# Which buffer a result may take, and the order of the last row tiles, in a one-core hybrid attention trunk

## The chip, the core and the metric

The kernel runs on one core of a Trainium2 chip. A core has five engines with a queue each: TensorE (PE; weight loads are shown apart as PEld), VectorE (DVE), ScalarE (ACT), GpSimd (POOL) and SyncE (SP). Here SP issues all loads and the stores of the output, and POOL issues the stores of intermediate results to DRAM. Each queue works in the order that the program gives it. Data lie in SBUF (128 partitions) and, for matmul results, in PSUM banks. The metric is the device time of one execution in microseconds (us); less is better. "Before" was timed in three runs, and one more execution was profiled.

## What is computed

One layer of a decoder trunk on 1024 tokens of 1024 channels, float32. A normalised input h goes through one wide projection, and its parts feed two recurrent branches, which are gated, merged and projected back:

```
h = rms_norm(x, norm_w) * (1 + scale) + shift          # scale, shift, gate from c
hq, hf, hi, hz, gq, gk, gv, gz, ga, mg = split(h @ w_in)
y_h = hgrn2_branch(hq, hf, hi, hz, ...)                # 8 heads of 128
y_g = gla_branch(gq, gk, gv, gz, ga, ...)              # 4 heads, keys 128, values 256
u_h, u_g = y_h @ w_branch[0], y_g @ w_branch[1]
merged = sigmoid(mg[0]) * u_h + sigmoid(mg[1]) * u_g
x = x + gate * (merged @ w_out)
out = rms_norm(x, final_norm_w)
```

Both branches are gated linear attentions, `S_t = diag(a_t) S_{t-1} + k_t v_t^T`, `o_t = S_t^T q_t`, computed in chunks.

## The kernel before

**Precision and slots.** Large matmuls run on pairs: each operand is split into a rounded high part (ACT, `copy` to fp32r) and the rest as low part (DVE, `tensor_sub`), and three products are summed (`split`, L195 to 202). Nearly everything large lives in 46 equal buffers of SBUF, 4 KB a partition each, which the class `Slots` hands out: loads, split parts, features, states. `get` takes the first slot of a heap; `free` puts a slot back with the running number of the takings as its key, so that the slot returned longest ago is taken first. A slot is returned when the program text is done with it, not when the hardware is: the framework then makes the next writer of that slot wait for whatever still reads or writes it. Some slots are returned right after the issue of a store that reads them; they are returned with `sent=True`, and in the last stages only (`S.behind = 8`, L1694) their key is put eight takings back. `Halves` (`Q`) hands out half slots.

**Order.** In the opening (up to `order.close()`, L450) TensorE, ACT and DVE work in the order of the text. Behind it the framework plans the order: it goes through the instructions by an estimate of its own and issues on each engine what is ready, the earlier in the text first. `tc.keep_in_program_order` ties an instruction behind the one that stands before it in the text on the same engine.

**Stages.**

- The opening: the norm of x, the modulation vector, and the first projections of GLA's queries and keys.
- The stream (`Stream`, L861; `stream.go()`, L1692): some 40 jobs, each a block of the input projection (`Feat`, L551; `Vblk`, L570; `Vblk2`, L614), in order. A job's weights are loaded two jobs ahead and split one ahead (`ahead`). Its result leaves PSUM through `silu_done` (L953, with L956 on ACT and L957 on DVE), `hf_done` (L1081) or copies of values (L609, L652). Between the matmuls of the jobs, `weave` places pieces of two side tracks: the attention of each head (`attention`, L661; keys turned into `kT`, L805 to 812; states, L833 to 840; outputs, L852 to 854; the square of the output, L985, and for GLA a row sum by matmul with ones, L961 to 972, L968 and L969), and preparation for the last stages: differences of the activations (`factors`, L1162) and sums of weight blocks (`weight_sums`, L1190: two loads x1 and x2 at L1196, two result slots s1 and s2 at L1199, four additions at L1202 to L1206, four stores on POOL at L1208). Finished GLA heads are scaled (L998) and stored by `put_act` (L918, L920).
- The last stages (`last_stages`, L1397, matmuls at L1351): gates and branch outputs by Strassen-like products of blocks (seven products per 2 x 2 block).
- The output stage (`out_stage`, L1585, matmuls at L1528): the output projection, again by seven products (1, 5, 3, 6, 7, 2, 4), each over four row tiles i. Row tiles 4 to 7 are closed behind product 7, row tiles 0 to 3 behind products 2 (first 512 columns) and 4 (last 512 columns).

**The end of a row tile.** `first_columns` sums the squares of the first half (ACT, accumulator into `sso[:, t, 0]`) and multiplies with the norm weight. `last_columns` (L1542) adds the product to the row (DVE, L1544), sums the squares of the second half (L1536), adds both sums (DVE, L1547), takes the root on ACT (L1548) and the reciprocal on DVE (L1549), then scales the first half on ACT (L1550) and the second on DVE (L1552), and stores both halves from SP (L1551, L1553). All of it for one tile stands in the text ahead of the next tile.

Of the kernel before, what the change touches and what calls it, by code (L numbers as in the profile page):

```python
# [10 lines left out]
F32 = mybir.dt.float32  # L11
# [24 lines left out]
class Slots:  # L36


    def __init__(self, pool, n):
        self.pool = pool  # L40
        self.free_list = [(-1, i - n, i) for i in range(n)]
        self.freed = self.behind = 0
        self.owner = {}
        self.serial = 0

    def get(self, shape, dtype=F32):
        i = heapq.heappop(self.free_list)[-1]
        self.serial += 1
        t = self.pool.tile([P] + list(shape), dtype, tag=f"s{i}", name=f"b{self.serial}")
        self.owner[id(t)] = (i, t)  # L50
        return t

    def free(self, *tiles, sent=False):
        for t in tiles:
            self.freed += 1
            heapq.heappush(self.free_list, (self.serial + (self.behind if sent else 0), self.freed, self.owner.pop(id(t))[0]))


# [29 lines left out]
def hybrid_trunk_kernel(  # L88
# [106 lines left out]
    def split(src, hi=None, lo=None):  # L195

        if hi is None:
            hi = S.get(list(src.shape[1:]), F32R)
            lo = S.get(list(src.shape[1:]), F32R)
        nc.scalar.copy(hi, src)  # L200
        nc.vector.tensor_sub(lo, src, hi.bitcast(F32))  # L201
        return hi, lo
# [326 lines left out]

    def split_feat(lw):  # L530
        raw, w = lw
        hi = S.get([KT, P], F32R)
        lo = S.get([KT, P], F32R)
        split(raw[:, :, 0:w], hi[:, :, 0:w], lo[:, :, 0:w])
        S.free(raw)
        return hi, lo
# [33 lines left out]
    class Vblk:  # L570
# [14 lines left out]
        def prep(self):  # L585
            self.wt = []
            for b in self.raw:
                hi = S.get([4, 256], F32R)
                lo = S.get([4, 256], F32R)
                split(b, hi, lo)  # L590
                self.wt.append((hi, lo))
                S.free(b)

        def run(self):
            v = [S.get([4, 256]) for _ in range(2)]
            for g in range(2):
                ps = dtile()
                for i in range(4):
                    t = g * 4 + i
                    for k in range(KT):  # L600
                        hi, lo = self.wt[k // 4]
                        lh, ll = h_hi[k][:, t * P:(t + 1) * P], h_lo[k][:, t * P:(t + 1) * P]
                        o = ps[:, i * 256:(i + 1) * 256]
                        nc.tensor.matmul(o, lh, hi[:, k % 4, :], start=(k == 0), stop=False)  # L604
                        nc.tensor.matmul(o, lh, lo[:, k % 4, :], start=False, stop=False)  # L605
                        nc.tensor.matmul(o, ll, hi[:, k % 4, :], start=False, stop=(k == KT - 1))  # L606
                        if k % 4 == 3:
                            yield
                nc.scalar.copy(v[g].rearrange("p a b -> p (a b)"), ps)  # L609
            for hi, lo in self.wt:  # L610
                S.free(hi, lo)
            self.done(v)

    class Vblk2:  # L614
# [18 lines left out]
                S.free(b)  # L633

        def run(self):
            v = [S.get([2, 512]) for _ in range(4)]
            for g in range(4):
                if g == 2:
                    self.middle()
                ps = dtile()  # L640
                for i in range(2):
                    t = 2 * g + i
                    o = ps[:, i * 512:(i + 1) * 512]
                    for k in range(KT):
                        hi, lo = self.wt[k // 2]
                        lh, ll = h_hi[k][:, t * P:(t + 1) * P], h_lo[k][:, t * P:(t + 1) * P]
                        nc.tensor.matmul(o, lh, hi[:, k % 2, :], start=(k == 0), stop=False)  # L647
                        nc.tensor.matmul(o, lh, lo[:, k % 2, :], start=False, stop=False)  # L648
                        nc.tensor.matmul(o, ll, hi[:, k % 2, :], start=False, stop=(k == KT - 1))
                        if k % 2:  # L650
                            yield
                nc.scalar.copy(v[g].rearrange("p a b -> p (a b)"), ps)  # L652
            for hi, lo in self.wt:
                S.free(hi, lo)
            self.done(v)
# [5 lines left out]
    def attention(q, k, f, v, vo, V, post, lead=3):  # L661
# [140 lines left out]
        yield 3.5  # L802


        kT = S.get([NCH, P])  # L805
        for g in range(2):
            nt = 4 if g == 0 else 3
            pt = mtile()
# [114 lines left out]
    def alpha_side():  # L923
        lower_bound()
        for h0 in (0, 2):
            zs = {}
            for h in (h0, h0 + 1):
                zb, m = S.get([T]), S.get([T])
                for th in range(2):
                    pz = mtile()  # L930
                    nc.tensor.matmul(pz, aw4[:, h * P:(h + 1) * P], ga4[:, th * 512:(th + 1) * 512],
                                     start=True, stop=True)
                    nc.scalar.activation(zb[:, th * 512:(th + 1) * 512], pz, AF.Identity,
                                         bias=vec[:, R_AB + h:R_AB + h + 1])
                tc.keep_in_program_order(nc.vector.tensor_scalar_min(m, zb, 0.0))
                nc.vector.scalar_tensor_tensor(zb, m, 2.0, zb, ALU.mult, ALU.subtract)
                zs[h] = zb
                alphas[h] = m
                yield 9 if h == 0 else 2
            for zb in zs.values():  # L940
                nc.scalar.activation(zb, zb, AF.Exp)
            yield 4
            for h, zb in zs.items():
                nc.scalar.activation(zb, zb, AF.Ln, bias=one_t)
                nc.vector.tensor_sub(alphas[h], alphas[h], zb)
            yield 4
            for h, zb in zs.items():
                nc.scalar.activation(alphas[h], alphas[h], AF.Exp, scale=1.0 / TAU)
                S.free(zb)
            yield 4  # L950
        S.free(ga4, aw4)

    def silu_done(store, key):  # L953
        def f(ps):
            s = S.get([T])
            nc.scalar.activation(s, ps, AF.Sigmoid)  # L956
            nc.vector.tensor_mul(s, s, ps)  # L957
            store[key] = s
        return f
# [14 lines left out]
    def gla_attention(h):  # L974
        qk = g_state
        v = qk.pop(("v", h))
        g = {}
        sq = {}

        def post(vh, half, po):  # L980
            if half == 0:
                g[vh] = qk.pop(("z", h, vh))
                sq[vh] = S.get([T])
            sl = slice(half * 512, half * 512 + 512)
            nc.scalar.activation(sq[vh][:, sl], po, AF.Square)  # L985
            nc.vector.scalar_tensor_tensor(g[vh][:, sl], po, vec[:, R_GN + vh:R_GN + vh + 1],
                                           g[vh][:, sl], ALU.mult, ALU.mult)

        yield from attention(qk.pop(("q", h)), qk.pop(("k", h)), alphas[h], lambda: v, 0, 256, post)
        S.free(*v)  # L990
        nc.vector.tensor_add(sq[0], sq[0], sq[1])
        yield 1.5
        rst = sq[1]
        yield from inverse_root(rst, sq[0], 256)
        for half in range(4):
            sl = slice(half * 256, half * 256 + 256)
            for vh in range(2):
                nc.vector.tensor_mul(g[vh][:, sl], g[vh][:, sl], rst[:, sl])  # L998
            yield 1.5
        for vh in range(2):  # L1000
            put_act(yg_d, 2 * h + vh, g[vh])
        S.free(*sq.values())

    def gla_k_done(h):
        def f(ps):
            t = S.get([T])
            nc.vector.tensor_copy(t, ps)
            g_state[("k", h)] = t
        return f
# [70 lines left out]

    def hf_done(h):  # L1081
        def fn(ps):
            f, k = S.get([T]), S.get([T])
            nc.scalar.activation(f, ps, AF.Sigmoid)
            nc.scalar.activation(k, ps, AF.Sigmoid, scale=-1.0)
            nc.vector.tensor_scalar(f, f, oml[:, h:h + 1], lb[:, h:h + 1], ALU.mult, ALU.add)
# [6 lines left out]
    def hgrn_attention(h):  # L1093
# [21 lines left out]
            S.free(sq[0])  # L1115
        if h == 7:
            yield 2
            rst = S.get([T])
            yield from inverse_root(rst, ssq[0], D)
            S.free(ssq[0])  # L1120
            rst_h[0] = rst
# [40 lines left out]
    def factors(acts, f):  # L1162
        sub = nc.vector.tensor_sub
        for kk in range(2):
# [1 line left out]
                yield 1  # L1166
            y = {}
            for b in ("12", "11", "22", "21"):
                y[b] = S.get([T])
                nc.sync.dma_start(y[b], part_of(acts, int(b[0]) - 1, int(b[1]) - 1, kk))  # L1170
            yield 6
            for p, dst, a, b in ((5, "11", "12", "11"), (7, "12", "12", "22"), (6, "22", "22", "11"), (4, "21", "21", "22")):
# [17 lines left out]
    def weight_sums(b, i):  # L1190
# [5 lines left out]
            nc.sync.dma_start(x.rearrange("p k a f -> p k (a f)"),  # L1196
                              src[kh * 512:(kh + 1) * 512, :].rearrange("(k p) f -> p k f", p=P))
        yield 6
        s1, s2 = S.get([2, 4, P]), S.get([2, 4, P])  # L1199
        parts = {5: s1[:, 0], 6: s1[:, 1], 3: s2[:, 0], 7: s2[:, 1]}  # L1200
        add = nc.vector.tensor_add
        add(parts[7], x1[:, :, 0], x1[:, :, 1])  # L1202
# [327 lines left out]

    nj = [0]

    def squares(t, f, src):
        nj[0] += 1
        junk = xb_f[:, nj[0] % 4 * 512:nj[0] % 4 * 512 + 512]
# [19 lines left out]
    def out_after(p, i):  # L1555
# [22 lines left out]
            Q.free(snap4.pop(i))  # L1578
        elif p == 2:
            first_columns(i, bank4["c", i])  # L1580
            R.free(bank4.pop(("c", i)))
        elif p == 4:
            last_columns(i, bank4["b", i])

    def out_stage():  # L1585
        for p in OUT_PRODUCTS:
# [141 lines left out]
```

## Time and profile before

| what | value |
|---|---|
| median of 3 runs | 1210.58 us (1209.76 to 1211.31) |
| the profiled execution's own time | 1208.55 us |
| its span, first to last instruction | 1206.8 us |
| granted TensorE clock, mean | 0.999 |
| DMA, mean over the span | 152 GB/s, 183.51 MB |
| SP's waits for a slot still in use, longest in total | 57.8 us (L1282, matmuls of L1351), 13 times |

All stretches named below are in us from the start of the span. A wait "A <- B" means that A's engine stood idle until B was done. In operand names the buffer numbers are left out: every slot is `b`, PSUM tiles are `pd`, `pm` and `sc_ps`; `yg`, `ws` and `fx` are DRAM copies of activations, weight sums and differences. The ends of matmuls are modelled, and idle time of an engine that isn't the bottleneck costs nothing by itself.

### The profile page before, as it was taken

To read this page: it belongs to the slowest core of one execution; us is meant where nothing else is said; L and a number is where in the kernel's file an instruction comes from. 1 tells how busy PE (TensorE), PEld (TensorE's weight loads), DVE (VectorE), ACT (ScalarE), POOL (GpSimd) and SP (SyncE) were. 2 spreads that over 40 slices of the span, in tenths; PEclk is the share of its full clock that TensorE was granted. 3 is DMA by queue.
4 is the path that set the end of the run, shared out by engine and by line. 5 is a ranking of instruction groups with operands and counts; after the bars stand their busy time and mean duration, and the time that the engine had idled before them with its cause. 6 is when DMAs were issued, how large, how long until landed. Compare 5 with 4: busy or idle time off the path is not lost.

```text
span 1206.8 us, 20832 instructions
## 1 busy us (share of the span) xinstructions
PE 1179.6 (98%) x8575; PEld 982.2 (81%) x8575; DVE 793.2 (66%) x1258; ACT 548.4 (45%) x798; POOL 95.2 (8%) x204
## 2 busy tenths in 40 slices
PE   5999999999999999999999999999999999999997
PEld 3777889889898888888888888877888888878886
DVE  5637444774947556877975365795653866988994
ACT  5646732434434244334333324464743644444554
POOL 4100000101101021011100000001120000000000
PEclk9999999999999999999999999999999999999999
DMA  9814000844444267255342212155797846435523
GB/s 323 278 70 140 18 19 19 292 146 159 158 152 153 59 206 255 93 175 170 121 175 54 70 36 71 36 175 168 248 349 248 279 155 209 125 107 172 177 101 124
DMA packets 130960, 183.51 MB, mean 152 GB/s; under 512 B 7467, under 2 KB 97633, under 8 KB 130866
## 3 DMA queue, kind: packets, MB, share of 16 engines
q1 hardware_dynamic: 117250, 136.87, 36.2%
q0 software_dynamic: 13568, 45.31, 9.7%
q8 instruction: 67, 1.10, 0.4%
q14 instruction: 27, 0.22, 0.1%
q10 hardware_dynamic: 48, 0.01, 0.0%
HBM read 132.87 MB, written 49.28 MB: 151 GB/s over the span
## 4 chain that ended last, share of the span: by engine, by line
PE 47%; issue 39%; POOL 3%; DMA 2%; DVE 2%; ACT 2%; SPq 0%; POOLq 0%; ACTq 0%; DVEq 0%
PE pd L1351 9%; PE pd L545 9%; PE sc_ps L1351 5%; PE pm L1351 5%; PE pd L1528 3%; PE pd L606 2%; PE pd L605 2%; PE pd L604 2%; POOL ws L1208 2%; PE sc_ps L1528 2%; DMA b<-in_w_in_dram 2%; PE pd L356 1%; PE pm L1528 1%; PE pm L852 1%; PE pm L854 1%
## 5 line engine op out<-in xcount | busy, mean ns | idle before, releaser
L545 PE MATMUL pd<-b,b 128*128 128x512 f32 x1632 | 387.4, 394 | 0.0
L545 PEld LDWEIGHTS pd<-b,b 128*128 128x128 f32 x1632 | 302.4, 188 | 64.8 <-issue 1.4
L1351 PE MATMUL pd<-b,b 128*128 128x512 f32 x720 | 173.6, 392 | 2.4 <-DVE b L957 1.0
L1351 PEld LDWEIGHTS pd<-b,b 128*128 128x128 f32 x720 | 133.9, 188 | 33.4 <-ACT b L1422 1.9
L201 DVE TENSOR_TENSOR b<-b,b 128x1024 fp32r<-128x1024 f32 (+2 forms) x90 | 97.9, 1097 | 71.1 <-ACT b L200 57.5
L200 ACT CAST b<-b 128x1024 fp32r<-128x1024 f32 (+2 forms) x90 | 84.2, 949 | 92.6 <-PE pd L545 13.7
L1294 DVE TENSOR_TENSOR b<-b,b 128x1024 fp32r<-128x1024 f32 x56 | 68.3, 1221 | 56.2 <-ACT b L1293 35.3
L1293 ACT CAST b<-b 128x1024 fp32r<-128x1024 f32 x56 | 58.7, 1051 | 64.6 <-PE pm L1351 20.0
L1351 PE MATMUL sc_ps<-b,b 128*128 128x512 f32 x324 | 79.3, 391 | 1.5 <-ACT scT L797 1.5
L604 PE MATMUL pd<-b,b 128*128 128x256 f32 x256 | 74.2, 290 | 0.0
L1351 PEld LDWEIGHTS sc_ps<-b,b 128*128 128x128 f32 x324 | 60.3, 188 | 15.1 <-ACT scT L797 1.9
L1272 DVE TENSOR_TENSOR b<-b,b 128x1024 fp32r<-128x1024 f32 x48 | 57.7, 1219 | 22.5 <-ACT b L1271 14.0
L606 PE MATMUL pd<-b,b 128*128 128x256 f32 x256 | 72.5, 283 | 0.0
L605 PE MATMUL pd<-b,b 128*128 128x256 f32 x256 | 72.4, 283 | 0.0
L1351 PE MATMUL pm<-b,b 128*128 128x512 f32 x300 | 72.1, 389 | 0.0
L1271 ACT CAST b<-b 128x1024 fp32r<-128x1024 f32 x48 | 49.9, 1051 | 36.6 <-PE pd L1351 16.0
L1351 PEld LDWEIGHTS pm<-b,b 128*128 128x128 f32 x300 | 56.3, 188 | 11.7
L356 PE MATMUL pd<-b,b 128*128 128x512 f32 x192 | 53.1, 409 | 1.8 <-ACT b L200 0.9
L1208 POOL DMA_DIRECT2D ws<-b x64 | 34.6, 540 | 224.8 <-DVE b L1202 121.7
L739 ACT COPY xb<-b 128x512 f32<-128x512 f32 x48 | 29.4, 620 | 48.9 <-PE sc_ps L719 26.8
L647 PE MATMUL pd<-b,b 128*128 128x512 f32 x128 | 51.2, 400 | 0.0
L648 PE MATMUL pd<-b,b 128*128 128x512 f32 x128 | 50.0, 390 | 0.0
(286 smaller groups left out, 1935.9 us busy)
## 6 DMA issues: line engine op xcount, KB each, us to landing
b<-in_w_in_dram SPq DMA_DIRECT2D x66, 512.0 KB, 4.3
ws<-b POOLq DMA_DIRECT2D x64, 256.0 KB, 3.4
b<-ws SPq DMA_DIRECT2D x32, 512.0 KB, 3.8
b<-in_x_dram SPq DMA_DIRECT2D x16, 512.0 KB, 5.7
b<-in_ada_w_dram SPq DMA_DIRECT2D x32, 256.0 KB, 7.0
b<-in_w_branch_dram SPq DMA_DIRECT2D x16, 512.0 KB, 4.2
b<-h SPq DMA_DIRECT2D x14, 512.0 KB, 4.2
wo<-b POOLq DMA_DIRECT2D x14, 512.0 KB, 4.9
```

The source lines that it names most:

```text
L200: nc.scalar.copy(hi, src)
L201: nc.vector.tensor_sub(lo, src, hi.bitcast(F32))
L356: nc.tensor.matmul(accs[f], wg(a, d, f), b[d][:, half * 512:half * 512 + 512], start=(d == 0 and n == 0), stop=(d == KT - 1 and n == 2))
L545: nc.tensor.matmul(ps[0:w, th * 512:(th + 1) * 512], a[:, k, 0:w], b[:, th * 512:(th + 1) * 512], start=(k == 0 and n == 0), stop=(k == KT ...
L604: nc.tensor.matmul(o, lh, hi[:, k % 4, :], start=(k == 0), stop=False)
L605: nc.tensor.matmul(o, lh, lo[:, k % 4, :], start=False, stop=False)
L606: nc.tensor.matmul(o, ll, hi[:, k % 4, :], start=False, stop=(k == KT - 1))
L1208: nc.gpsimd.dma_start(w_sums[b][i // 2][q][:, i % 2 * 512:i % 2 * 512 + 512], parts[p].rearrange("p k f -> p (k f)"))
L1293: nc.scalar.copy(hi, t)
L1294: nc.vector.tensor_sub(lo, t, hi.bitcast(F32))
L1351: nc.tensor.matmul(o, a[:, sl], c, start=(p in (1, 5) and kt == 0 and n == 0), stop=(kt == 3 and n == 2), skip_group_check=True)
L1528: nc.tensor.matmul(o, a, b, start=(p in (1, 5) and kt == 0 and n == 0), stop=(kt == 3 and n == 2), skip_group_check=True)
```

## The change

It has two parts; the opening is untouched.

**Slots.** `get` has a new argument `written`. Without it, it takes the head of the list as before. With it, it takes the first slot of the list that was not returned with a store during the last eight takings (`sent` keeps, for each slot, the running number at its last such return), and the head if there is none. The argument is given where an engine writes a result into the slot, not where a load does: parts of `split`, `split_feat` and `Vblk.prep`, values, `kT`, the gates of GLA, `silu_done`, squares, keys, `hf_done`, the root of HGRN2, the sums s1 and s2, and the four tiles of `factors` (which are loaded, then overwritten).

**The end.** Row tiles 0 to 3 are closed by `close_columns` and `close_rows` in place of `last_columns` (tiles 4 to 7 keep it). The first sum of squares is turned into `sum / D + EPS` during product 2, and ACT's root takes it as its bias, with the second sum scaled by 1/D. The scaling and the stores of a tile (`close_rows`) stand behind the next tile's addition; that of tile 2 stands ahead of tile 3's.

```diff
-    def get(self, shape, dtype=F32):
-        i = heapq.heappop(self.free_list)[-1]
+    def get(self, shape, dtype=F32, written=False):
+        entry = self.free_list[0]
+        if written:
+            entry = next((e for e in sorted(self.free_list) if self.serial - self.sent.get(e[-1], -99) > 8), entry)
+        self.free_list.remove(entry)
+        heapq.heapify(self.free_list)
+        i = entry[-1]
         self.serial += 1
...
     def free(self, *tiles, sent=False):
         for t in tiles:
             self.freed += 1
+            if sent:
+                self.sent[self.owner[id(t)][0]] = self.serial
...
     def split(src, hi=None, lo=None):
 
         if hi is None:
-            hi = S.get(list(src.shape[1:]), F32R)
-            lo = S.get(list(src.shape[1:]), F32R)
+            hi = S.get(list(src.shape[1:]), F32R, written=True)
+            lo = S.get(list(src.shape[1:]), F32R, written=True)
...
-        s1, s2 = S.get([2, 4, P]), S.get([2, 4, P])
+        s1, s2 = S.get([2, 4, P], written=True), S.get([2, 4, P], written=True)
...
+    def close_rows(t):
+        r = xr[t][:, 512:1024]
+        rs = rso[:, t:t + 1]
+        nc.scalar.activation(xr[t][:, 0:512], xr[t][:, 0:512], AF.Copy, scale=rs)
+        nc.sync.dma_start(o2[t * P:(t + 1) * P, 0:512], xr[t][:, 0:512])
+        tc.keep_in_program_order(
+            nc.vector.scalar_tensor_tensor(r, r, rs, fnw[0][:, 512:1024], ALU.mult, ALU.mult))
+        nc.sync.dma_start(o2[t * P:(t + 1) * P, 512:1024], r)
+
+    def close_columns(t, bank):
+        r = xr[t][:, 512:1024]
+        if t == 3:
+            close_rows(2)
+        tc.keep_in_program_order(nc.vector.tensor_add(r, r, bank))
+        if t in (1, 2):
+            close_rows(t - 1)
+        squares(t, 1, r)
+        rs = rso[:, t:t + 1]
+        nc.scalar.activation(rs, sso[:, t, 1:2], AF.Sqrt, bias=sso[:, t, 0:1], scale=1.0 / D)
+        nc.vector.reciprocal(rs, rs)
+        if t == 3:
+            close_rows(3)
...
             first_columns(i, bank4["c", i])
+            nc.vector.tensor_scalar(sso[:, i, 0:1], sso[:, i, 0:1], 1.0 / D, EPS, ALU.mult, ALU.add)
             R.free(bank4.pop(("c", i)))
         elif p == 4:
-            last_columns(i, bank4["b", i])
+            close_columns(i, bank4["b", i])
```

More of the change, by code (lines that the diff above doesn't have):

```diff
@@ L42, in __init__ @@
         self.freed = self.behind = 0
+        self.sent = {}
         self.owner = {}
         self.serial = 0
-    def get(self, shape, dtype=F32):
-        i = heapq.heappop(self.free_list)[-1]
+    def get(self, shape, dtype=F32, written=False):
[5 more added lines that the diff above has]
+        i = entry[-1]
         self.serial += 1
@@ L531, in split_feat @@
         raw, w = lw
-        hi = S.get([KT, P], F32R)
-        lo = S.get([KT, P], F32R)
+        hi = S.get([KT, P], F32R, written=True)
+        lo = S.get([KT, P], F32R, written=True)
         split(raw[:, :, 0:w], hi[:, :, 0:w], lo[:, :, 0:w])
@@ L587, in prep @@
             for b in self.raw:
-                hi = S.get([4, 256], F32R)
-                lo = S.get([4, 256], F32R)
+                hi = S.get([4, 256], F32R, written=True)
+                lo = S.get([4, 256], F32R, written=True)
                 split(b, hi, lo)
@@ L594, in run @@
         def run(self):
-            v = [S.get([4, 256]) for _ in range(2)]
+            v = [S.get([4, 256], written=True) for _ in range(2)]
             for g in range(2):
@@ L635, in run @@
         def run(self):
-            v = [S.get([2, 512]) for _ in range(4)]
+            v = [S.get([2, 512], written=True) for _ in range(4)]
             for g in range(4):
@@ L802, in attention @@
         yield 3.5
-        kT = S.get([NCH, P])
+        kT = S.get([NCH, P], written=True)
         for g in range(2):
@@ L927, in alpha_side @@
             for h in (h0, h0 + 1):
-                zb, m = S.get([T]), S.get([T])
+                zb, m = S.get([T], written=True), S.get([T], written=True)
                 for th in range(2):
@@ L954, in f @@
         def f(ps):
-            s = S.get([T])
+            s = S.get([T], written=True)
             nc.scalar.activation(s, ps, AF.Sigmoid)
@@ L982, in post @@
                 g[vh] = qk.pop(("z", h, vh))
-                sq[vh] = S.get([T])
+                sq[vh] = S.get([T], written=True)
             sl = slice(half * 512, half * 512 + 512)
@@ L1005, in f @@
         def f(ps):
-            t = S.get([T])
+            t = S.get([T], written=True)
             nc.vector.tensor_copy(t, ps)
@@ L1082, in fn @@
         def fn(ps):
-            f, k = S.get([T]), S.get([T])
+            f, k = S.get([T], written=True), S.get([T], written=True)
             nc.scalar.activation(f, ps, AF.Sigmoid)
@@ L1117, in hgrn_attention @@
             yield 2
-            rst = S.get([T])
+            rst = S.get([T], written=True)
             yield from inverse_root(rst, ssq[0], D)
@@ L1168, in factors @@
             for b in ("12", "11", "22", "21"):
-                y[b] = S.get([T])
+                y[b] = S.get([T], written=True)
                 nc.sync.dma_start(y[b], part_of(acts, int(b[0]) - 1, int(b[1]) - 1, kk))
```

## The prediction

> **What bounds the kernel now.** I read the page's head first, then the busy time of each engine by stage, then the list of what TensorE waited for. Quoted are the head, four of seven windows (window; length; then busy us and count of PE, weight loads, DVE, ACT, POOL; granted clock; DMA share; GB/s), and six rows of PE's waits (total, times, longest, in us).
>
> ```profile
> span 1206.8 us, 20832 instructions
> PE 1179.6 (98%) x8575; PEld 982.2 (81%) x8575; DVE 793.2 (66%) x1258; ACT 548.4 (45%) x798; POOL 95.2 (8%) x204
> 0.00:113.00 113.00, 97.75 (x474) 70.86 (x474) 60.91 (x119) 66.94 (x110) 23.09 (x70) 1.00 0.64 212
> 281.00:640.00 359.00, 358.50 (x3209) 305.05 (x3209) 254.03 (x462) 142.70 (x212) 45.27 (x84) 1.00 0.49 158
> 805.00:1123.00 318.00, 314.45 (x1564) 257.49 (x1565) 220.91 (x255) 158.12 (x207) 17.16 (x32) 1.00 0.61 201
> 1199.30:1206.80 7.50, 0.00 (x1) 0.00 (x0) 2.37 (x5) 2.40 (x5) 0.00 (x0) 0.83 0.37 141
> PE pm L223 <- DVE b L214: 6.8, 4, 3.7
> PE sc_ps L1351 <- ACT scT L797: 1.5, 1, 1.5
> PE pd L1351 <- DVE b L957: 1.0, 1, 1.0
> PE pd L1351 <- ACT b L1422: 0.8, 2, 0.5
> PE pd L1351 <- DVE b L1443: 0.4, 1, 0.4
> PE pm L833 <- ACT b L812: 0.4, 1, 0.4
> ```
>
> TensorE is the bound: it is idle for 1206.8 - 1179.6 = 27.2 us. Of these 113.00 - 97.75 = 15.3 lie in the opening, which the change leaves alone, and 7.5 behind the last matmul. The remaining 4.4 us lie between: 0.5 in 281 to 640 us, 3.6 in 805 to 1123, 0.4 in the windows not shown. The last five rows name 4.1 us of these 4.4. So anything the change frees on ACT, DVE or the load queue before the end is worth at most about 4 us, and at the end at most what can be cut from the 7.5.
>
> **The change, part 1: the end.** This is the timeline of the last row tiles (start, duration, engine, line, operation; the bracket is idle time and what ended it). The three PE rows end with the matmuls of row tiles 0, 2 and 3 of product 4 (the first, of 24, ends with tile 0's; tile 1's isn't shown); among them is DVE's product of product 2 (L1540). Below the additions (L1544) of tiles 0 and 2 stand tile 2's scaling (L1552) and the chain of tile 3. The last two rows are from the opening: a square with its accumulator read and the root (L209) that reads the accumulator directly.
>
> ```profile
> 1185.54 5.60 PE L1528 MATMUL pd<-b,b 128*128 128x512 f32 x24
> ...
> 1186.52 0.69 DVE L1540 TENSOR_TENSOR b<-sc_ps,b 128x512 f32<-128x512 f32 x1 [2.03 <-ACT xb L1536]
> ...
> 1191.18 0.69 DVE L1544 TENSOR_TENSOR b<-b,pd 128x512 f32<-128x512 f32 x1 [1.25 <-PE pd L1528]
> ...
> 1193.70 2.88 PE L1528 MATMUL sc_ps<-b,b 128*128 128x512 f32 x12
> ...
> 1196.42 2.88 PE L1528 MATMUL pd<-b,b 128*128 128x512 f32 x12
> ...
> 1197.01 0.68 DVE L1544 TENSOR_TENSOR b<-b,sc_ps 128x512 f32<-128x512 f32 x1
> ...
> 1199.25 0.75 DVE L1552 SCALAR_TENSOR_TENSOR b<-b,rso,b 128x512 f32<-128x512 f32 x1
> 1199.91 0.68 DVE L1544 TENSOR_TENSOR b<-b,pd 128x512 f32<-128x512 f32 x1
> ...
> 1200.68 0.63 ACT L1536 ACTIVATE xb<-b 128x512 f32<-128x512 f32 x1 [0.71 <-DVE b L1544]
> 1201.21 0.19 ACT L1536 ACTIVATION_READ_ACCUMULATOR xb<-b 128x1 f32 x1
> 1201.43 0.16 DVE L1547 TENSOR_TENSOR rso<-sso 128x1 f32<-128x1 f32 x1 [0.84 <-ACT xb L1536]
> 1201.62 0.29 ACT L1548 ACTIVATE rso<-rso,eps_t 128x1 f32<-128x1 f32 x1 [0.23 <-DVE rso L1547]
> ...
> 1202.15 0.75 DVE L1552 SCALAR_TENSOR_TENSOR b<-b,rso,b 128x512 f32<-128x512 f32 x1
> ...
> 1203.32 0.38 SPq L1553 DMA_DIRECT2D out_dram<-b  x1
> ...
> 10.34 0.19 ACT L207 ACTIVATION_READ_ACCUMULATOR b<-b 128x1 f32 x1
> 10.56 0.29 ACT L209 ACTIVATE rsx<-ssx,eps_t 128x1 f32<-128x1 f32 x1
> ```
>
> Removed: the addition L1547 between the two sums of squares, once per tile of product 4. From accumulator read to root it takes 1201.62 - 1201.21 = 0.41 us; where the root reads the accumulator itself it takes 10.56 - 10.34 = 0.22. That is 0.19 us less in every tile's chain. Added for it: four 128x1 operations on sso during product 2. The nearest row is L1547 at 0.16 us, so 0.6 us on DVE, one in each gap like the 2.03 us ahead of L1540; the next tile's matmuls cover it. Without cover it would cost that 0.6.
>
> Moved: the scaling of tile t goes behind the addition of tile t+1, and only that of tile 2 stays ahead of addition 3. Before, tile 3's matmuls end at 1196.42 + 2.88 = 1199.30, but its addition starts at 1199.91: the scaling of tile 2 started at 1199.25 and held DVE. Tile 2's matmuls end at 1193.70 + 2.88 = 1196.58, its addition starts at 1197.01, 0.43 late for the same reason; the delay has been handed from tile to tile.
>
> After: addition 2 starts at 1196.62 (0.04 behind the matmul, as tile 0 has it, where nothing is in the way: 1191.18 against 1185.54 + 5.60 = 1191.14). The chain from addition to scaling is 1202.15 - 1199.91 = 2.24 us now, so 2.05 without L1547. Tile 2's scaling starts at 1196.62 + 2.05 = 1198.67. The next addition follows a scaling by 1199.91 - 1199.25 = 0.66, so DVE is free for addition 3 at 1199.33; its matmul allows 1199.30 + 0.04 = 1199.34. I take 1199.35 instead of 1199.91: 0.56 gained. Tile 1's scaling, now behind addition 2, runs from 1197.3 to 1198.0 while ACT squares tile 2, and is done before 1198.67. Part 1: 0.56 + 0.19 = 0.75 us. What follows (reciprocal, scaling, both stores, 1206.8 - 1203.32 = 3.5 us of landing and closing) is the same. Every result store is still issued on SP in row order, and nothing else is queued there.
>
> [...] The rows 1199.25 and 1199.91 agree that the addition does not pass the scaling.
>
> **Part 2: the slots.** The order of takings and returns does not change, since the room it asks for is a count. I wrote down the order that the code gives (855 takings) and applied both rules: only 12 results pass over a slot at the head of the list, and counting the shifts that follow 25 takings get a slot with another history, the first near 281 us, the last near 640. Behind the stream `S.behind` = 8 already puts slots with stores eight takings back, and I find none changed there. So of PE's five waits above, those in the last stages (L797, L957, L1422, L1443: 3.7 us) keep their slots.
>
> Of the 25, three matter for times:
>
> ```profile
> DVE b L201 <- PE pd L606: 6.6, 1, 6.6
> SPq L1196 <- DMA ws<-b: 18.1, 5, 10.5
> 333.87 0.69 DVE L1202 TENSOR_TENSOR b<-b 128x512 f32<-128x512 f32 x1 [0.32 <-DMA b<-in_w_in_dram]
> 350.94 0.75 DVE L986 SCALAR_TENSOR_TENSOR b<-pm,vec,b 128x512 f32<-128x512 f32 x1 [5.85 <-ACT b L985]
> 350.95 0.39 PE L854 MATMUL pm<-b,b 128*128 128x128 f32 x2
> 355.78 1.22 DVE L201 TENSOR_TENSOR b<-b,b 128x1024 fp32r<-128x1024 f32 x1 [1.17 <-ACT b L200]
> 358.37 0.39 PE L968 MATMUL pm<-b,ones_r 128*128 128x512 f32 x1
> 424.51 0.37 SPq L527 DMA_DIRECT2D b<-in_w_in_dram  x1
> 436.30 1.07 POOL L920 DMA_DIRECT2D yg<-b  x2 [0.27 <-DVE b L998]
> 439.38 1.22 DVE L201 TENSOR_TENSOR b<-b,b 128x1024 fp32r<-128x1024 f32 x1 [2.31 <-DMA yg<-b]
> 446.28 1.06 ACT L200 CAST b<-b 128x1024 fp32r<-128x1024 f32 x1 [0.83 <-PE pd L648]
> ws<-b POOLq DMA_DIRECT2D x64, 256.0 KB, 3.4
> ```
>
> (a) The low part of a weight (439.38) no longer waits 2.3 us for the store of yg: its slot is one whose readers are done. DVE gains the 2.3; PE does not wait there (0.5 us idle in the whole window), so 0.
>
> (b) The weight sum at 333.87 gets a slot that held a query of GLA, read by PE until 351.34 (350.95 + 0.39). Its four additions (at most 4 x 0.69 = 2.8 us) move behind that, where DVE still has idle time (1.17 us before 355.78; the 5.85 before 350.94 lie too early). They cannot stay where they are: the state updates behind them on DVE feed the very matmul. Waiting behind them are their four stores on POOL and the loads into the two input slots; those sums are needed hundreds of us later. Against that, a load of value weights that waited for the same query can go earlier. PE notices only if the root at 358.37 comes late. Its split (355.78) ends at 357.00, cover 1.37 us. From below 0, from above 2.8 - 1.37 = 1.4 us; I take 0, because the additions are short and fall into gaps one by one.
>
> (c) The load at 424.51 gets a slot that a store of yg reads. The last of the two stores issued from 436.30 to 437.37 lands 3.4 us (the row of stores) after about 436.8, at 440.2. So the load, and every load behind it on SP, can be held for 15.7 us. Its cast is at 446.28, and loads from w_in land in a few us, so it arrives with about 2 us over; the sums fed by the next loads shift by as much. Taken as 0, at most about 1 us.
>
> [...] The row of SP's 18.1 us behind ws stores agrees that SP stands still for them. [...]
>
> **The sum.** 1208.55 us is the profiled execution's own time, 1.75 above its span. 1208.55 - 0.75 = 1207.80. The median of the runs shown is 2.03 higher, so 1210.58 - 0.75 = 1209.83: I say 1209.8.
>
> **The rivals.** Slower: DVE is held by (b). If the sums go ahead of the root's split, PE stands for 1.4 us at 358.37, and the time is 1209.83 + 1.4 = 1211.2; if DVE is held as long as its longest wait for a slot that PE reads (the 6.6 of the row with L606), 6.6 - 1.37 = 5.2 us, 1215.0. It decides from 1.37 + 0.75 = 2.1 us ahead of the split. For it: the planner of orders doesn't know real times, and 6.6 happened. Against: that 6.6 didn't reach PE.
>
> Faster: freeing slots earlier also removes PE's waits. If the wait for L812 goes, 1209.4; if all 4.1 us go, 1205.7. For it: ACT's copy into kT (L812) is now a marked result. Against: the rows name ACT and DVE work, not stores, and four of five lie where no slot changes.
>
> The change doesn't do what it says: the scaling of tile 2 or the new order on ACT holds addition 3 as before. Then 0.19 is left, 1210.4, or nothing, 1210.6.
>
> **How the numbers follow.** Forecast 0.53; slower by (b) 0.17, of it 0.12 over 2.4 us; faster by PE's waits 0.18, of it 0.14 beyond 2.4 us; nothing at the end 0.12. 0.2% is 2.4 us, about what a measurement of this kernel can tell from no change. So faster 0.14, same 0.74, slower 0.12. The runs shown scatter by 0.8 either way. With that, and with the cheap halves of both rivals, the range is 1207.8 to 1211.9, and about 0.1 is left out on each side.
>
> **What would show it.** No L1547 behind product 4; the last addition within 0.1 us of 1199.30, counted from the last matmul's end, instead of 0.61; accumulator read to root 0.22; span from that matmul's end 6.75 us, not 7.5. The weight sum of 333.87 behind 351; a load held on SP until about 440. PE idle between 281 and 640 us still near 0.5, and the same waits after 805. I am wrong if PE shows new waits in that stretch, above all for L201 or the root's matmuls, or if additions behind 1199.3 still queue behind scalings.

## The result and the profile after

| | before | after |
|---|---|---|
| median | 1210.29 us (1209.17 to 1211.31, 6 runs) | 1215.3 us (1214.8 to 1216.1, 6 runs) |
| the profiled execution's own time | 1208.55 us | 1214.8 us |
| its span | 1206.8 us | 1213.1 us |

The changed kernel is slower: the ratio is 1.0043, with a 95% interval of 1.003 to 1.0056. The forecast was 1209.8 us, with a range of 1207.8 to 1211.9. Of all executions below only one, of e_hold_short, was slow (1975.57 us, at a mean granted clock of 0.56), and it is left out of that run's median and ratio. From line 195 of the kernel before on, up to the new functions at the end, line numbers are 8 higher now: L747 is L755, L811 is L819, L833 is L841, L1196 is L1204, L1203 is L1211.

The head, four windows by stage (columns as before the change) and five of TensorE's waits of the changed kernel; the waits left out lie in the opening and the last stages, as before the change:

```profile
span 1213.1 us, 20829 instructions
PE 1182.4 (97%) x8575; PEld 983.6 (81%) x8575; DVE 792.9 (65%) x1258; ACT 548.1 (45%) x798; POOL 95.6 (8%) x204
113.00:281.00 168.00, 164.06 (x1427) 145.19 (x1426) 92.87 (x152) 70.76 (x93) 6.98 (x13) 0.99 0.28 93
281.00:640.00 359.00, 357.73 (x3228) 305.23 (x3227) 248.26 (x457) 141.93 (x212) 44.92 (x83) 1.00 0.49 157
...
805.00:1123.00 318.00, 314.84 (x1623) 257.14 (x1622) 221.41 (x254) 160.88 (x210) 17.22 (x32) 1.00 0.61 204
1206.39:1213.10 6.71, 0.00 (x1) 0.00 (x0) 1.64 (x4) 1.79 (x5) 0.00 (x0) 0.86 0.45 170
PE pm L819 <- DVE b L755: 2.9, 1, 2.9
PE pm L841 <- ACT b L820: 1.1, 2, 0.6
PE pm L1078 <- DVE b L209: 0.8, 1, 0.8
PE sc_ps L782 <- DVE blk L771: 0.6, 1, 0.6
PE sc_ps L727 <- DVE tot L730: 0.6, 1, 0.6
```

The stretch behind the last matmul has become shorter, 6.71 us for 7.50. What is lost lies ahead of it: the last matmul ended at 1199.30 us and ends at 1206.39 now, 7.1 us later. The window 113 to 281 is the worst. TensorE is idle there for 168.00 - 164.06 = 3.9 us, and the same window of the kernel before has next to none:

```profile
113.00:281.00 168.00, 167.98 (x1475) 149.45 (x1474) 93.61 (x153) 72.25 (x95) 6.42 (x12) 1.00 0.28 92
```

One wait makes up most of it, the transposes of the keys (L819) behind DVE's product on k (L755): 2.9 us, once. Here is DVE's timeline around it, first in the kernel before, then in the changed one:

```profile
253.41 0.16 DVE L750 TENSOR_TENSOR tot<-tot 128x8 f32<-128x8 f32 x1
...
254.75 0.67 DVE L747 TENSOR_TENSOR b<-b,tot 128x512 f32<-128x512 f32 x1
...
282.81 0.69 DVE L1203 TENSOR_TENSOR b<-b,b 128x512 f32<-128x512 f32 x1 [0.41 <-PE pm L854]
```

```profile
253.67 0.16 DVE L758 TENSOR_TENSOR tot<-tot 128x8 f32<-128x8 f32 x1
259.61 0.69 DVE L1211 TENSOR_TENSOR b<-b,b 128x512 f32<-128x512 f32 x1 [5.77 <-DMA b<-in_w_in_dram]
260.21 0.68 DVE L755 TENSOR_TENSOR b<-b,tot 128x512 f32<-128x512 f32 x1
```

An addition of the first weight sum (L1203, now L1211), whose result is needed hundreds of us later, stood at 282.81. It now stands directly ahead of the product, and DVE waits 5.77 us for its load. The product moves from 254.75 to 260.21 with it. The addition could move because two things that it needs came earlier. One is its load, seen in SP's loads for that sum (start, duration of the group up to its last issue, line, count), before and after:

```profile
254.12 13.77 SPq L1196 DMA_DIRECT2D b<-in_w_in_dram  x2
```

```profile
248.21 0.38 SPq L1204 DMA_DIRECT2D b<-in_w_in_dram  x1
...
254.10 37.05 SPq L1204 DMA_DIRECT2D b<-in_w_in_dram  x3
```

Before, the two loads were issued at 254.12 and at 254.12 + 13.77 - 0.37 = 267.5 us. Now they are issued at 248.21 and 254.10: the second has a slot that is free 13.4 us earlier. It landed only when DVE could go on, just before 259.61, some 5.5 us after its issue.

The other is its result slot. Before, its load had been issued 15 us earlier, and yet the addition waited at 282.81 for TensorE's L854, as its line shows: the slot of s1 was still read by the attention. The sum's first addition (L1202, now L1210), which needs only the first load and writes into s2, is the comparison, before and after:

```profile
280.80 0.69 DVE L1202 TENSOR_TENSOR b<-b 128x512 f32<-128x512 f32 x1 [4.28 <-PE pm L852]
```

```profile
286.26 0.69 DVE L1210 TENSOR_TENSOR b<-b 128x512 f32<-128x512 f32 x1 [4.27 <-PE pm L860]
```

Its load, too, goes earlier now (248.21 for 254.12), but by the order of the takings s2 keeps its slot (taking 171), and this addition has not moved: it still waits for the attention, and is 5.46 us later like TensorE itself. s1 (taking 170) got another slot, and the addition that writes into it moved. So the load alone did not do it. How much each of the two contributes was not measured, since no run changes one without the other.

The order of DVE's instructions is fixed when the kernel is built; the planner that made it evidently counted the load as landed by then. Its own estimate isn't in the trace, and the experiments below test what follows from it. In the 12 us up to 258 the DMA engines were full in the changed kernel (rows: window, length, busy times, granted clock, DMA share, GB/s):

```profile
246.00:258.00 12.00, 11.38 (x155) 9.02 (x153) 7.56 (x18) 5.00 (x6) 1.47 (x3) 1.00 1.01 335
...
262.00:263.00 1.00, 1.00 (x8) 1.00 (x7) 1.00 (x3) 0.95 (x5) 0.00 (x0) 0.63 0.36 139
263.00:264.00 1.00, 1.00 (x7) 1.00 (x6) 1.00 (x3) 0.98 (x4) 0.00 (x0) 0.50 0.00 0
264.00:265.00 1.00, 1.00 (x6) 1.00 (x6) 0.96 (x3) 0.98 (x3) 0.00 (x0) 0.50 0.00 0
265.00:266.00 1.00, 1.00 (x7) 1.00 (x7) 1.00 (x2) 0.98 (x2) 0.00 (x0) 0.66 0.00 0
```

The last four rows are the second part of the loss. After TensorE's stand its granted clock is 0.5 for about 0.74 + 1 + 1 + 0.68 = 3.4 us (a window's mean of 0.63 is 0.74 us at half clock). What each step cost is read from the same instructions in both kernels: TensorE's transposes, the last split-product matmul ahead of the states, and the first matmuls of the states, before and after.

```profile
257.66 0.93 PE L811 MATMUL pm<-ident,b 128*128 128x128 f32 x7
...
261.17 0.28 PE L606 MATMUL pd<-b,b 128*128 128x256 f32 x1
261.29 0.91 PE L833 MATMUL pm<-b,b 128*128 128x256 f32 x3
```

```profile
260.95 0.98 PE L819 MATMUL pm<-ident,b 128*128 128x128 f32 x7 [2.87 <-DVE b L755]
...
266.02 0.28 PE L614 MATMUL pd<-b,b 128*128 128x256 f32 x1
266.75 1.56 PE L841 MATMUL pm<-b,b 128*128 128x256 f32 x6 [0.45 <-ACT b L820]
```

The differences are 3.29, 4.85 and 5.46 us. So the stand brought about 3.0 (at 252 us, ahead of it, TensorE was already 0.3 late), the half clock 1.56, and ACT, which is late with the keys after it, 0.6: some 5.5 of the 7.1 us by 267. The rest comes in small waits later on (L727 and L1078 above are the largest). One of them is at the place of the prediction's (c), at 456 us:

```profile
444.71 0.37 SPq L535 DMA_DIRECT2D b<-in_w_in_dram  x1
446.49 0.37 SPq L1204 DMA_DIRECT2D b<-in_w_branch_dram  x1
...
451.67 0.69 DVE L1211 TENSOR_TENSOR b<-b,b 128x512 f32<-128x512 f32 x1 [9.80 <-DMA b<-in_w_branch_dram]
...
456.29 0.37 DVE L730 TENSOR_TENSOR tot<-tot 128x64 f32<-128x64 f32 x1
...
456.69 0.89 PE L727 MATMUL sc_ps<-xb,b 128*32 128x48 f32 x64 [0.61 <-DVE tot L730]
```

The load that was issued at 424.51 is held on SP until 444.71, the next load with it, and an addition on DVE stands 9.80 us for that one (4.03 us before the change, at 444.63). TensorE loses 0.6 us.

The end of the changed kernel, as it was shown of the one before:

```profile
1203.51 2.88 PE L1536 MATMUL pd<-b,b 128*128 128x512 f32 x12
...
1205.72 0.75 DVE L1547 SCALAR_TENSOR_TENSOR b<-b,rso,b 128x512 f32<-128x512 f32 x1
1206.43 0.69 DVE L1554 TENSOR_TENSOR b<-b,pd 128x512 f32<-128x512 f32 x1
...
1207.91 0.29 ACT L1559 ACTIVATE rso<-sso 128x1 f32<-128x1 f32 x1
```

The last matmul ends at 1203.51 + 2.88 = 1206.39, and the last addition starts 0.04 us behind it (0.61 before).

### The profile page after: what moved, and what is told of

The parts are those of the page before. It is cut to its first block, busy times and chain, and to the rows that moved or that the text cites. A ratio compares the mean times of both kernels' runs of the same rounds, so it can differ in the third digit from the quotient of the medians.

```text
span 1213.1 us, 20829 instructions
## 1 busy us (share of the span) xinstructions
PE 1182.4 (97%) x8575; PEld 983.6 (81%) x8575; DVE 792.9 (65%) x1258; ACT 548.1 (45%) x798; POOL 95.6 (8%) x204
## 4 chain that ended last, share of the span: by engine, by line
issue 54%; PE 34%; POOL 4%; DMA 3%; DVE 2%; ACT 1%; SPq 1%; POOLq 0%; DVEq 0%; ACTq 0%
PE pd L1359 9%; PE sc_ps L1359 5%; PE pm L1359 5%; PE pd L1536 3%; PE pd L553 3%; POOL ws L1216 2%; PE sc_ps L1536 2%; PE pm L1536 1%; DMA xb<-in_w_in_dram 1%; DMA b<-in_w_in_dram 1%; PE pd L614 1%; PE pd L613 1%; PE pd L612 1%; PE pd L364 1%; POOL yh L928 1%
## 5 line engine op out<-in xcount | busy, mean ns | idle before, releaser
L209 DVE TENSOR_TENSOR b<-b,b 128x1024 fp32r<-128x1024 f32 (+2 forms) x90 | 98.0, 1100 | 71.7 <-ACT b L208 54.0
L747 ACT COPY xb<-b 128x512 f32<-128x512 f32 x48 | 29.4, 620 | 50.4 <-PE sc_ps L727 25.3
```

## The experiments

Theory 1: the slots pull a load ahead (by the lines above they free a sum's result slot as well), one addition of a weight sum is then planned ahead of a product that TensorE needs, and DVE, in order, stands for the load; the end by itself is a gain. All times are medians; each ratio is to the kernel before, run on the same chip beside it.

| run | what it is | median, us | ratio, 95% interval |
|---|---|---|---|
| e_end | new end, old slots | 1208.67 | 0.9985 [0.9977, 0.9994] |
| e_slots | new slots, old end | 1216.85 | 1.0052 [1.0038, 1.0066] |
| e_first | new end, new rule for takings 162 to 170 alone | 1214.3 | 1.0032 [1.0023, 1.0042] |
| e_rest | new end, new rule from taking 171 on | 1209.85 | 0.9996 [0.9987, 1.0006] |
| e_first_pin | e_first, two additions of the first sum tied | 1208.77 | 0.9986 [0.9977, 0.9996] |
| e_pin_all | whole change, two additions of every sum tied | 1210.66 | 1.0004 [0.9994, 1.0013] |
| e_end_pin | e_end, two additions of every sum tied | 1211.62 | 1.0013 [1.0004, 1.0022] |
| e_hold_long, e_hold_short | e_end, DVE held at the first head | 1210.27, 1211.05 | 0.9998 [0.9989, 1.0007], 1.0004 [0.9995, 1.0014] |
| e_hold2_long, e_hold2_short | e_end, DVE held at the second head | 1210.2, 1209.64 | 1.0002 [0.9993, 1.0012], 0.9995 [0.9986, 1.0004] |

**The two parts apart.** Against the changed kernel, e_end is

```diff
-        if written:
+        if written and False:
```

> The new closing of the row tiles alone; every slot is handed out as before. All theories: the end gains what the changed kernel shows there (last matmul's end to the end of the span 6.7 us instead of 7.5), so 1210.3 - 0.8 = 1209.5, and PE waits after the opening as before, about 4 us in all. Were the closing part of the loss, it would come out above 1210.3.

and e_slots keeps the rule and closes the tiles as before:

```diff
-            nc.vector.tensor_scalar(sso[:, i, 0:1], sso[:, i, 0:1], 1.0 / D, EPS, ALU.mult, ALU.add)
...
-            close_columns(i, bank4["b", i])
+            last_columns(i, bank4["b", i])
```

> The new slots alone, the old closing. All theories: the changed kernel plus the 0.8 us of the closing, 1216.1; last matmul's end to the end of the span 7.5 us.

The end alone takes 1208.67 - 1210.2 = -1.5 us, the slots alone 1216.85 - 1210.2 = +6.7 (the kernel before, run beside them, took 1210.2). Their sum, 5.1 us before rounding, is what the whole change costs (1215.3 - 1210.29 = 5.0): all of the loss belongs to the slots.

**Which slots.** The rule is limited to the takings around the first weight sum, or to all later ones:

```diff
-        if written:
+        if written and 162 <= self.serial + 1 <= 170:
```

```diff
-        if written:
+        if written and self.serial + 1 > 170:
```

> The new closing, and the new rule for takings 162 to 170 alone (nine slots, all between 250 and 290 us). Theory 1 (a load that gets its slot earlier lets the planner put an addition of a weight sum ahead of the attention's products on DVE, where it waits for the landing): PE loses nearly everything here, 3 us of wait at 261 us, then 1.5 to 2 us at half clock and behind it, so 1209.5 + 5.5 = 1215.0. Theory 2 (loads held on SP behind stores): the loss lies in the other takings, so 1209.5 to 1210.

> The new closing, and the new rule for all takings but the first 170 (16 slots, from 326 to 640 us). Theory 1: no wait at 261 us; left are 0.7 us near 450 us and some tenths later, so 1209.8 to 1211. Theory 2: the load that waits for a store near 440 us holds the queue and with it DVE and PE, so about 1215.

DVE in e_first, and TensorE's wait there; then the granted clock in its windows:

```profile
260.25 0.69 DVE L1211 TENSOR_TENSOR b<-b,b 128x512 f32<-128x512 f32 x1 [6.51 <-DMA b<-in_w_in_dram]
260.86 0.69 DVE L755 TENSOR_TENSOR b<-b,tot 128x512 f32<-128x512 f32 x1
```

```profile
PE pm L819 <- DVE b L755: 3.3, 1, 3.3
```

```profile
261.00:262.00 1.00, 0.40 (x2) 0.40 (x3) 1.00 (x2) 0.00 (x0) 0.54 (x1) 0.84 0.03 8
262.00:263.00 1.00, 1.00 (x8) 1.00 (x6) 1.00 (x4) 0.54 (x3) 0.00 (x0) 0.50 0.65 254
...
265.00:266.00 1.00, 1.00 (x10) 1.00 (x9) 1.00 (x2) 0.96 (x3) 0.00 (x0) 0.95 0.00 0
```

The rule at nine takings out of 855 brings the wait, the half clock and 1214.3 - 1208.67 = 5.6 us over the end alone. All later takings together bring 1.2 us over it by the medians, with intervals that overlap, and no wait at 261.

**The order alone.** e_first_pin has the slots and the loads of e_first. Only the first two additions of that one sum are tied to the order of the program:

```diff
-        add(parts[7], x1[:, :, 0], x1[:, :, 1])
-        add(parts[5], x1[:, :, 1], x2[:, :, 1])
+        if (b, i) == (0, 0):
+            tc.keep_in_program_order(add(parts[7], x1[:, :, 0], x1[:, :, 1]))
+            tc.keep_in_program_order(add(parts[5], x1[:, :, 1], x2[:, :, 1]))
+        else:
...
```

> The new closing and the nine changed slots of takings 162 to 170, and the first two additions of the first weight sum are tied behind the DVE instruction ahead of them in the text, so that the planner can't move them up. Loads and slots are those of the run with the nine slots alone (1214.3). Theory 1 (an addition moved up on DVE waits for the load's landing): no wait of 3 us at 261 us, no half clock, 1208.7 to 1209.5. Rival (the earlier load itself, or its traffic, makes the attention late): the wait stays, about 1214.

SP's loads, and DVE (the second addition is at L1212 in this kernel):

```profile
248.47 0.38 SPq L1204 DMA_DIRECT2D b<-in_w_in_dram  x1
...
253.33 34.93 SPq L1204 DMA_DIRECT2D b<-in_w_in_dram  x3
```

```profile
255.17 0.68 DVE L755 TENSOR_TENSOR b<-b,tot 128x512 f32<-128x512 f32 x1
...
281.84 0.69 DVE L1212 TENSOR_TENSOR b<-b,b 128x512 f32<-128x512 f32 x1
```

The loads are as early as in the changed kernel, the product is back at 255.17, and the time is that of the end alone (1208.77 against 1208.67). So neither the early load nor its traffic costs anything; the place of the addition does. This decides for theory 1 as far as the price goes. It does not show why the planner moved the addition, since load and result slot are early in both kernels.

**Tying all of them**, in the changed kernel (e_pin_all) and with the old slots (e_end_pin):

```diff
-        add(parts[7], x1[:, :, 0], x1[:, :, 1])
-        add(parts[5], x1[:, :, 1], x2[:, :, 1])
+        tc.keep_in_program_order(add(parts[7], x1[:, :, 0], x1[:, :, 1]))
+        tc.keep_in_program_order(add(parts[5], x1[:, :, 1], x2[:, :, 1]))
```

> The whole change, with the first two additions of every weight sum tied behind the DVE instruction ahead of them in the text. Theory 1: the wait at 261 us and the half clock are gone; the smaller losses from 326 us on may stay, so 1208.9 to 1210.5. Rival: still 1214 to 1215.

> The new closing, the old slots, and the first two additions of every weight sum tied to the order of the program. Theory 1: with the old slots no weight sum stands ahead of a product that TensorE needs, so tying has nothing to save: 1208.7, like the new closing alone. Rival (the tied order is better by itself, and that is what brought the two tied runs back to the closing's time): 1207.5 or less.

With all sums tied the whole change takes 1210.66 us, a little over what was expected, and the wait at 261 is gone. With the old slots tying costs 1211.62 - 1208.67 = 3.0 us, where nothing was expected. (The profiled spans differ by 3.1 us, 1210.1 for 1207.0; 1.1 of it is there at 22 us, in the opening, which tying does not touch.) So a tied order isn't better by itself (the rival falls), and it seems to have a price of its own. Where that comes from was not taken apart. TensorE's largest new wait in e_end_pin:

```profile
383.63 0.89 PE L727 MATMUL sc_ps<-xb,b 128*32 128x48 f32 x64 [1.31 <-DVE tot L730]
```

Ahead of it DVE's splits (L209) stood for stores, 1.06 us for yg at 375.58 and 1.29 us for ws at 378.09, and not at a tied addition.

**A hold of known length.** A reduction on DVE whose result nobody reads (it repeats a slice of the scores 42 or 33 times, 5.75 or 4.55 us) is put directly ahead of the product, which is tied behind it, in a kernel with the new end and the old slots:

```diff
+        if me == 1:
+            nc.vector.reduce_max(out=wga[:, 0, 0:1], in_=sc_ps[:, 640:768].unsqueeze(1).to_broadcast([P, 42, P]),
+                                 axis=mybir.AxisListType.XY)
...
-        grow(64)
+        grow(64, me == 1)
```

> The new closing, slots as before; in the first head a maximum over 42 x 128 elements (its result is not used; it overwrites one number that nothing reads afterwards) stands on DVE right ahead of the attention's product that stood behind the waiting addition. It holds DVE for some 5.5 us without any load. Theory 1: the product starts some 5.2 us late, its cover is 2.6 us, PE waits about 2.6 us at 260 us, then runs at half clock for 3.4 us, so 1208.7 + 4 to 5 = 1213. Were only the wait counted and not the clock: 1211.3. Rival (the loads' traffic matters): no loss, 1208.7.

> As the one before with 33 x 128 elements, some 4.4 us on DVE. The product starts some 4.0 us late, PE waits about 1.4 us. If the clock falls only behind a longer pause: clock 1.0 throughout, 1208.7 + 1.4 = 1210.1. If a pause of this length is enough: 1208.7 + 3 = 1211.7.

Both missed, because the reduction ran at 186 us: the head near 254 is the second, not the first. With `me == 2`:

> The new closing with the old slots, plus a DVE reduction of 5.75 us (that is what it took in the earlier run, where it fell at the first head, at 186 us) directly ahead of the second head's last product on k, L755, near 254 us. In the run of the new closing alone that product ends at 254.80 and TensorE reaches the transposes that read it at 257.35, so 2.49 us of a hold are covered: TensorE should stand for 0.06 + 5.75 - 2.55 = 3.3 us. Theory 1 (a stand of about 3 us costs itself and then a stretch at half clock of 3.4 us, some 1.6 us more, as after 261 us in the changed kernel): a stretch of half clock shows, 1208.7 + 3.3 + 1.6 = 1213.6. Rival (the stand costs its length alone; the half clock of the changed kernel has another cause): no half clock, 1212.0.

> The same with a reduction of 4.55 us: TensorE stands for 4.55 - 2.49 = 2.1 us. Theory 1, if the stand must be near 3 us to bring the half clock: no half clock, 1208.7 + 2.1 = 1210.8. If a stand of 2 us brings it too: 1212.4.

DVE and TensorE in e_hold2_long, where L755 is the product and L824 the transposes:

```profile
255.98 5.75 DVE L798 TENSOR_REDUCE wga<-sc_ps 128x1 f32<-128x5376 f32 x1
261.64 0.70 DVE L755 TENSOR_TENSOR b<-b,tot 128x512 f32<-128x512 f32 x1
```

```profile
258.93 0.28 PE L612 MATMUL pd<-b,b 128*128 128x256 f32 x1
...
262.39 0.98 PE L824 MATMUL pm<-ident,b 128*128 128x128 f32 x7 [0.43 <-DVE b L755]
```

Neither theory's number came. The product is later here (261.64) than in the changed kernel (260.21), yet TensorE waits 0.43 us for it, not 2.87. The order has the split-product matmuls (from 258.93) ahead of the transposes here; evidently the planner counted the reduction. In the changed kernel it left the transposes in front, and TensorE stood. So a late product isn't by itself what costs; between these two runs it is whether the order was made for the delay. For the clock these runs say nothing, since TensorE stood for this product for only 0.43 us, and 0.28 us in e_hold2_short.

## Why the prediction was wrong, step by step

- **The bound.** Right: the last matmul ends 7.1 us later, and the time follows it.
- **Part 1, the end.** Right in mechanism and about right in size. The addition starts 0.04 us behind the matmul, as said; from the accumulator's read to the root it takes 0.22 us; the span from the last matmul's end is 6.71 us, where 6.75 was forecast. That is 7.50 - 6.71 = 0.79 us for the 0.75 of the sum. The medians of e_end give 1.5 us, its ratio an interval of 0.7 to 2.8.
- **Part 2, the failed step.** The text held that a load which "can go earlier" is no loss, and asked of each changed slot only whether it comes free too late. Of the 25 changed slots it took three to matter for times, and those of the first weight sum were not among them. It put the first changed slot "near 281 us", where that sum's additions stood, while the loads into its slots are issued at 248 to 254 us. The runs showed that with an earlier load and an earlier result slot the planner places an addition ahead of the attention's product, and that the load then lands after the point the order was made for: 5.77 us of DVE, 2.87 of TensorE, then half clock. The sum had 0 for this; the nine takings around it cost 5.6 us (e_first).
- **(a)** The wait of 2.3 us for the store of yg ahead of the low part is gone, and it was worth nothing, as said.
- **(b)** Right that it costs TensorE nothing: no wait of the root's matmuls is in its list. Three of the four additions moved behind the query's last read, as said (333.87 went to 357.10, the last from 336.46 to 362.36); the one into the other result slot stayed (334.87, now 339.42).
- **(c)** The held load came (until 444.71, said 440.2; the whole kernel is 5.5 us late there), and loads behind it were held too. The "few us" in which loads from w_in land are 4.3 by the median of the 66 of 512 KB on the page of the kernel before. It was taken as 0 and at most about 1 us; TensorE lost 0.6 us at 456. The margin was smaller than counted because the load that DVE stood for was one held behind it.
- **The rivals.** The slower one had the right kind, DVE held in order by a weight sum's addition, up to 1215.0 us. It had the wrong place (358 instead of 254) and the wrong trigger (a slot that comes late instead of a load and a slot that come early). That its 1215.0 lies next to the measured 1215.3 is luck. It was given 0.17, and its own test, the 1.37 us of cover ahead of one split, was made at that one place alone. "The planner of orders doesn't know real times" stood in the text as a reason for it; it should have been applied to every instruction that a changed slot or load may move.
- **Later waits.** The rest, 7.1 - 5.5 = 1.6 us by the trace, is the sum of small waits from 450 us on, with one gain between them: the wait for scT in the last stages is 0.3 us, for 1.5 before. So two of the signs named did not come as said: TensorE's idle time from 281 to 640 us is 1.3 us instead of 0.5, and the waits after 805 are not quite the same. With the rule from taking 171 on (e_rest) the median is 1.2 us over the end alone; which of these waits makes it up was not taken apart, and 1.5 of the 2.5 us between the two profiled spans (1209.5 and 1207.0) are already there at the end of the opening.

The best versions are the end alone (1208.67) and the end with the nine slots and one tied sum (1208.77). They can't be told apart, so the new slots bring nothing here.

## What to carry to other kernels

Where a planner fixes each engine's order when the kernel is built, an earlier load, or a result slot that comes free earlier, is not a gain for certain: look for what it can now put ahead on the engine that consumes it, and who waits behind that. An engine that runs in order should never wait for a transfer ahead of work that the bounding engine needs soon (here DVE stood 5.77 us for one load, and TensorE 2.87 us behind it); tie such a filler down to its late place, but only that one: tying all of them came out 3.0 us slower here where there was nothing to save. Compare the two built orders before comparing times: of 855 takings of slots nine mattered, and one instruction that had moved explained most of the loss.

## What the hardware showed beside it

After a stand of TensorE of 2.87 us its granted clock fell to 0.5 for 3.4 us, which cost 1.56 us more; after one of 3.3 us in e_first the windows from 261 to 266 us give 0.32 + 1 + 1 + 1 + 0.10 = 3.4 us at half clock too. The length of a stand alone did not decide it here: behind the wait of 3.7 us in the opening of the kernel before (L223, up to 7.35 us) the windows 7 to 9 and 9 to 12 us have a clock of 1.00, and so has the whole opening in the rows shown with the prediction. The stand of 1.31 us in e_end_pin left the clock alone (window, length, busy times, clock):

```profile
379.00:384.00 5.00, 3.69 (x48) 2.83 (x50) 4.93 (x13) 0.31 (x1) 0.00 (x0) 1.00 0.33 92
384.00:388.00 4.00, 4.00 (x66) 3.32 (x52) 3.90 (x9) 0.62 (x1) 1.03 (x2) 1.00 0.06 20
```

What brings the half clock on is not shown. No run here separates its price from that of the stand, since TensorE waited for the product behind the holds that were meant to do so for only 0.43 us (e_hold2_long) and 0.28 us (e_hold2_short).
